# A 16384 x 2048 by 2048 x 2048 product on one Trainium2 core: the head joins the table of places, SBUF is divided by hand, chained products run by column halves

## The chip, the core and the metric

The kernel runs on one core of a Trainium2 chip. The core has five engines that run their own instruction streams: TensorE (PE, with its weight loads shown as PEld), VectorE (DVE), ScalarE (ACT), GpSimd (POOL) and SyncE (SP), which here issues nearly all DMAs. The metric is the device time of one execution in microseconds; lower is better.

## The reference

```python
def reference(x, w):          # x: 8 x 2048 x 2048, w: 2048 x 2048, float32
    cs = np.cumsum(x, axis=1)
    diff = cs - np.concatenate([np.zeros(...), cs[:, :-1, :]], axis=1)
    return np.matmul(diff, w).astype(np.float32)
```

The difference of a running sum is x again, so what is computed is x times w, with x as 16384 rows of 2048.

## The kernel before

The rows of x are 128 tiles of 128 rows. The work has a head, 31 groups of four tiles, and an end.

**The head** (lines 197 to 473) multiplies the first four tiles (PLAIN = 4) in bfloat16, directly, while w arrives. w comes in 32 slices of 128 x 1024 float32 (512 KB): `w.0.k` is the first column half of rows 128k and on, `w.1.k` the second. The four tiles of x come in 16 blocks of 256 KB, quarter q of the columns for tile r. Each quarter is cast to bfloat16 (`cast_x`, DVE), turned by 16 transposes on PE (`turn_x`) and copied to `xP` (`turned`). Each slice of w is cast into a ring of seven buffers (`taken`, ACT), and DVE takes its largest absolute value (1.21 us each). A product is one 128x128 by 128x512 matmul. The first half of w has 112 of them (7 for each k), the second 128, and `left_over` 16: one bank's worth of the result is left to the end of the head, since there are only eight banks in PSUM and the transposes need one. Ahead of all this, 7 dummy products (WARM) run on zeros. The results go from PSUM to buffers of the pool `o` (`plain_out`) and out by DMA: seven of the first half on GpSimd's queue behind the maximum over all partitions (L296), the others on SP.

When the whole of w is there, its maximum gives a scale, `uinv` (L381), and w is rewritten in place as float16 blocks: B11, B12, B21 (`block`, L392), later B22, and the differences T1 = B12 - B11, T2 = B22 - T1, T3 = B22 - B12, T4 = B21 - T2. They are operands of Winograd's form of the 2 x 2 block product, which has seven products instead of eight.

**A group** handles tiles g, g+1, g+2, g+3. Each tile is loaded in two halves (`load`, 512 KB each), weighed (`weigh`, ACT, for its scale; `mean` and `scale` on DVE, `unit` on POOL), narrowed to float16 (`narrow`, ACT) and turned by two DMA transposes (`turn`). DVE makes the sums S1 to S4. Group 0 (`group_plain`) and group 1 are special; groups 2 to 30 are alike and have 204 products each: 64 in chained products (`S2g T2`, `S2h T2`, `S3g T3`, `S3h T3`, each of 16 products that add to a pair of banks, X or Y) and five second-level products P1 to P5 of seven `slot`s (`P1.0` to `P1.6`, four products each; class `Quarters`). Within such a P, ACT copies a bank after slot 0 (`first`), slot 2 (`out2`) and slot 4 (`out4`), and DVE adds it to another (`middle`, `last`). Some right operands of the second level (Q1, Q3, Q4) pass through a buffer `flow`, filled by DVE or by DMA from a copy in DRAM. Results leave PSUM by `keep` (ACT) and `add` (DVE), and then by `put` (DMA, 512 KB).

**What sets the order.** Operations of the groups are not issued at once: `record` files each under its period (group) and a label, and `emit(places)` sorts all by `period * PERIOD + place` and then issues them. `after` ties every instruction of PE, DVE, ACT, SP and POOL to the one issued before it on the same engine, so each engine runs them in the order of the table, and waits for operands where they are late. The label's number is the role: `put2.1` is half 1 of tile g+2, `load7.1` half 1 of the next group's fourth tile, `put-1.0` the half that the group before left. The table has four columns: groups 0, 1, 2, and one for all others. The head is not in it: its instructions are issued as the code calls them, with an `emit()` between.

Memory is taken from pools: `ring`, `o` and `first` for the head, closed at its end, then `C`, `inner`, `flow` and `chain` over the same memory. An operation that first writes a new pool's buffer waits for what used those bytes in the old one.

Of the kernel before, what the change touches and what calls it, by code (L numbers as in the profile page):

```python
# [10 lines left out]
def kernel(  # L11
# [29 lines left out]
    WARM = 7  # L41
# [3 lines left out]
    PERIOD = 833  # L45
# [16 lines left out]
    uw = const.tile([P, 1], f32, name="uw")  # L62
    uinv = const.tile([P, 1], f32, name="uinv")

    waste = const.tile([P, NH], mybir.dt.uint8, name="waste")
    F = const.tile([P, 4, NH], f32, name="F")
# [3 lines left out]
    sums_at, means_at, scales_at, units_at = (  # L70
        [const.tile([P, n], f32, name=f"{name}{i}") for i in range(count)]
        for name, n, count in (("m", 2, 4), ("m1_", 1, 2), ("s", 1, 8), ("u", 1, 8))
    )
# [5 lines left out]
    def bank(i):  # L79
        return banks[i]  # L80
# [3 lines left out]
    def after(engine, ask):  # L84
        if engine in last:
            with tc.issue_after(last[engine].ins):
                said = ask()
        else:
            said = ask()
        last[engine] = said[-1] if isinstance(said, tuple) else said  # L90
        return said

# [104 lines left out]
    with tc.tile_pool(name="ring", bufs=7) as ring, tc.tile_pool(  # L197
        name="o", bufs=7
    ) as opool, tc.tile_pool(name="first", bufs=1) as first:
        xP = first.tile([P, PLAIN, KO, P], bf16, name="xP")  # L200
        eye = first.tile([P, P], bf16, name="eye")
        wmax = first.tile([P, 2 * KO], f32, name="wmax")
        wred = first.tile([P, 1], f32, name="wred")
        zeros = xP[:, 0, :KQ, :].rearrange("p k m -> p (k m)")


        def resting(k, a):
            return whole[k][:, a, 1, :]


        number = [resting(i, 1)[:, :P] for i in range(3)]
        nc.vector.memset(zeros, 0.0)
        nc.vector.memset(number[0], 1.0)
        nc.vector.tensor_tensor_scan(
            number[1], number[0], number[0], 0.0, MUL, ADD
        )
        nc.vector.transpose(number[2], number[1])
        for i in range(0, P, 32):
            own = ds(i, 32)
            nc.vector.tensor_scalar(  # L220
                eye[own, :],
                number[1][own, :],
                number[2][own, i : i + 1],
                None,
                mybir.AluOpType.is_equal,
            )

        def load_x(q, rows=range(PLAIN)):
            for r in rows:
                nc.sync.dma_start(  # L230
                    resting(KH - 1 - q, r // 2)[:, ds(r % 2 * NB, NB)],
                    x2[ds(r * P, P), ds(q * KQ * P, KQ * P)],
                )

        def cast_x(q, pairs=range(2)):
            xb = resting(q, 0).bitcast(bf16).rearrange("p (a c) -> p a c", a=2)
            for a in pairs:
                after(
                    "dve",
                    lambda: nc.vector.tensor_copy(xb[:, a], resting(KH - 1 - q, a)),  # L240
                )
            return xb


        def turn_x(xb, a, i):
            v = bank(i).bitcast(bf16)
            for k in range(2 * KQ):
                at = ds(k * P, P)
                after("pe", lambda: nc.tensor.transpose(v[:, at], xb[:, a, at], eye))
            return v  # L250

        def turned(q, a, v, engine):
            to = xP[:, ds(2 * a, 2), ds(q * KQ, KQ), :].rearrange("p r k m -> p r (k m)")
            v = v.rearrange("p (r c) -> p r c", r=2)
            if engine == "act":
                after("act", lambda: nc.scalar.copy(to, v))
            else:
                after("dve", lambda: nc.vector.tensor_copy(to, v))

        wb = {}  # L260

        def fetch(h, ko):
            wt = whole[ko % KH][:, ko // KH, h, :]
            nc.sync.dma_start(wt, w[ds(ko * P, P), ds(h * NH, NH)])

        def taken(h, ko):
            wt = whole[ko % KH][:, ko // KH, h, :]
            i = h * KO + ko
            b = wb[h, ko] = ring.tile([P, NH], bf16, name="wb")
            after("act", lambda: nc.scalar.copy(b, wt))  # L270
            after(
                "dve",
                lambda: nc.vector.tensor_reduce(
                    wmax[:, i : i + 1], wt, AX.X, MAX, apply_absolute_value=True
                ),
            )


        def here(h, r):
            return range(1 if h == 0 and r == PLAIN - 1 else 2)  # L280

        def plain(h, r, ko):
            for n in here(h, r):
                after(
                    "pe",
                    lambda: nc.tensor.matmul(  # L286
                        ps[r][n],
                        xP[:, r, ko, :],
                        wb[h, ko][:, ds(n * NB, NB)],
                        start=(ko == 0),  # L290
                        stop=(ko == KO - 1),
                    ),
                )

        def put(c, rows, columns, queue=nc.gpsimd):
            return queue.dma_start(out2[rows, columns], c)  # L296

        def plain_out(h, r):
            for n in here(h, r):
                if h == 0 or r > 0:  # L300
                    c = opool.tile([P, NB], f32, name="o")
                else:
                    c = ring.tile([P, NH], bf16, name="wb").bitcast(f32)
                after("act", lambda: nc.scalar.copy(c, ps[r][n]))  # L304
                done.append((c, ds(r * P, P), ds(h * NH + n * NB, NB)))


        for i in range(WARM):
            after(
                "pe",  # L310
                lambda: nc.tensor.matmul(
                    bank(0), zeros[:, :P], zeros, start=True, stop=True
                ),
            )
        AHEAD = 3
        done = []
        ps = [[bank(2 * r + n) for n in here(0, r)] for r in range(PLAIN)]


        loads = {2: 1, 5: 2, 9: 3}  # L320
        turns = {2: (1, 0), 3: (1, 1), 5: (2, 0), 6: (2, 1), 9: (3, 0), 10: (3, 1)}
        for ko in range(KO):
            if ko in loads:
                load_x(loads[ko])
            if ko < 2:
                load_x(0, range(2 * ko, 2 * ko + 2))
            fetch(0, ko)
        for ko in range(KO - KQ):
            if ko == 0:
                for a in range(2):  # L330
                    xb = cast_x(0, [a])
                    turned(0, a, turn_x(xb, a, 6 + a), "dve")
                    if a == 0:
                        taken(0, ko)
                    for r in (2 * a, 2 * a + 1):
                        plain(0, r, ko)
                continue
            if ko in turns:
                q, a = turns[ko]
                if a == 0:  # L340
                    xb = cast_x(q)
                v = turn_x(xb, a, 7)
                taken(0, ko)
                turned(q, a, v, "act")
            else:
                taken(0, ko)
            for r in range(PLAIN):
                plain(0, r, ko)
        for ko in range(KO - KQ, KO):
            taken(0, ko)  # L350
        for ko in range(AHEAD):
            fetch(1, ko)
        for ko in range(AHEAD):
            taken(1, ko)
        for r in range(PLAIN):
            for ko in range(KO - KQ, KO):
                plain(0, r, ko)
            plain_out(0, r)
        ps = [[bank(2 * r + n) for n in here(1, r)] for r in range(PLAIN)]
        for ko in range(KO - KQ):  # L360
            if ko >= AHEAD:
                fetch(1, ko)
                taken(1, ko)
            for r in range(PLAIN):
                plain(1, r, ko)
        for ko in range(KO - KQ, KO):
            fetch(1, ko)
        for ko in range(KO - KQ, KO):
            taken(1, ko)


        for t in (PLAIN, PLAIN + 2):
            load(t, 0)
            load(t, 1)
        emit()
        after("dve", lambda: nc.vector.tensor_reduce(wred, wmax, AX.X, MAX))
        whole_max = nc.gpsimd.partition_all_reduce(uw, wred, P, bass_isa.ReduceOp.max)
        after(
# [962 lines left out]
```

## Time and profile before

| | |
|---|---|
| median of three runs | 1460.88 us (1459.04 to 1462.82) |
| the profiled execution | 1460.01 us, span 1458.2 us |
| HBM read, written | 196.61 MB, 135.79 MB |
| DMA, busy share over the span, mean rate | 0.93 for the main queue, 273 GB/s |

A span runs from the first to the last instruction. Of each engine the profile has the busy time and, for each instruction, what released it. DMA rows show their issue on SP's queue (`SPq`); the landing is a separate time. In the table by stage, the first column is the stretch in us from the span's start.

### The profile page before, as it was taken

How to read it: one execution, taken by the hardware profiler on the slowest of the kernel's cores; microseconds unless marked ns; L12 is line 12 of the kernel's file. 1: busy time of each engine (PE TensorE's matmuls, PEld its weight loads, DVE VectorE, ACT ScalarE, POOL GpSimd, SP SyncE). 2: the span in 40 equal slices, each digit the busy share in tenths (PEclk: the TensorE clock that was granted, in tenths of full speed). 3: DMA queues.
4: the chain of work that ended last, by engine and by line, in shares of the span. 5: the costliest groups of instructions: out<-in, count | busy, mean ns of one | idle time of the engine just before them, and what ended most of it. 6: DMA issues, size and time to landing. Idle time of an engine off the chain costs nothing.

```text
span 1458.2 us, 20418 instructions
## 1 busy us (share of the span) xinstructions
PE 1440.1 (99%) x6677; PEld 652.3 (45%) x6683; DVE 1260.6 (86%) x2292; ACT 1142.9 (78%) x1742; POOL 42.8 (3%) x136
## 2 busy tenths in 40 slices
PE   8999999999999999999999999999999999999997
PEld 3444444444444444444444444444444444444443
DVE  7898988888888888888888888888888988888886
ACT  5887778887888877888878788878788878888863
POOL 0100000000000000000000000000000000000000
PEclk9999999999999999999999999999999999999999
DMA  9989999899999999999999999999999999999983
GB/s 360 367 221 264 278 271 258 281 307 250 276 273 261 281 302 261 271 270 267 286 288 267 265 275 268 296 280 265 263 276 269 306 263 277 257 269 279 313 230 125
DMA packets 355387, 398.79 MB, mean 273 GB/s; under 512 B 272272, under 2 KB 272784, under 8 KB 355152
## 3 DMA queue, kind: packets, MB, share of 16 engines
q1 hardware_dynamic: 354720, 395.65, 93.4%
q0 software_dynamic: 560, 1.84, 0.3%
q8 instruction: 52, 0.85, 0.2%
q14 instruction: 55, 0.45, 0.1%
HBM read 196.61 MB, written 135.79 MB: 228 GB/s over the span
## 4 chain that ended last, share of the span: by engine, by line
PE 93%; DMA 3%; DVE 1%; ACT 1%; issue 0%; SPq 0%; DVEq 0%; POOL 0%; ACTq 0%
PE b L541 61%; PE b L522 31%; DMA W<-in_w_dram 3%; PE b L286 1%; DVE W L392 1%; DMA out_dram<-c 1%; ACT W L577 0%; DVE c L566 0%; DMA out_dram<-o 0%; ACT o L304 0%; ACT c L555 0%; DVE b L509 0%; DVE x L509 0%; ACT xP L160 0%; ACT wb L270 0%
## 5 line engine op out<-in xcount | busy, mean ns | idle before, releaser
L522 PE MATMUL b<-W,x 128*128 128x512 f16 x2176 | 524.0, 379 | 0.0
L566 DVE SCALAR_TENSOR_TENSOR c<-b,u,c 128x512 f32<-128x512 f32 x612 | 444.9, 744 | 42.1 <-PE b L541 25.6
L541 PEld LDWEIGHTS <-inner 128*128 128x128 f16 x2700 | 264.0, 98 | 318.8 <-DVE inner L509 0.4
L541 PE MATMUL b<-W,inner 128*128 128x512 f16 x1640 | 401.9, 379 | 0.0
L555 ACT ACTIVATE c<-b,u 128x512 f32<-128x512 f32 x496 | 321.5, 687 | 29.4 <-PE b L541 9.2
L522 PEld LDWEIGHTS <-x 128*128 128x128 f16 x2176 | 212.9, 98 | 257.1 <-issue 0.7
L160 ACT ACTIVATE F<-F,s 128x1024 f16<-128x1024 f32 x246 | 282.6, 1149 | 48.9 <-DVE s L149 45.9
L541 PE MATMUL b<-W,x 128*128 128x512 f16 x1180 | 293.5, 379 | 0.3 <-ACT b L558 0.3
L128 ACT ACTIVATE waste<-F 128x1024 uint8<-128x1024 f32 x246 | 260.0, 1057 | 35.3 <-DMA F<-in_x_dram 34.1
L541 PEld LDWEIGHTS <-x 128*128 128x128 f16 x1416 | 138.6, 98 | 167.5 <-issue 0.6
L558 ACT COPY chain<-b 128x512 f32<-128x512 f32 x234 | 136.6, 584 | 93.0 <-PE b L541 91.6
L541 PE MATMUL b<-flow,inner 128*128 128x512 f16 x704 | 180.7, 379 | 0.0
L509 DVE TENSOR_TENSOR b<-b,chain 128x512 f32<-128x512 f32 x234 | 162.1, 693 | 14.9 <-ACT c L555 11.2
L558 ACT COPY b<-b 128x512 f32<-128x512 f32 x147 | 83.8, 570 | 77.4 <-PE b L541 38.7
L509 DVE TENSOR_TENSOR inner<-x,x 128x1024 f16<-128x1024 f16 (+1 forms) x180 | 91.9, 511 | 27.8 <-PE b L541 26.1
L509 DVE TENSOR_TENSOR flow<-W 128x2048 f16<-128x2048 f16 x90 | 109.6, 1218 | 0.0
L509 DVE TENSOR_TENSOR x<-x,x 128x1024 f16<-128x1024 f16 x124 | 84.8, 686 | 3.1
L541 PE MATMUL b<-inner 128*128 128x512 f16 x356 | 86.5, 379 | 0.0
L150 POOL TENSOR_SCALAR u<-m,uw 128x1 f32<-128x1 f32 x124 | 37.8, 312 | 1307.2 <-DVE m L147 1299.2
L509 DVE TENSOR_TENSOR inner<-inner 128x512 f16<-128x512 f16 x116 | 49.3, 425 | 30.0 <-PE b L541 27.9
L509 DVE TENSOR_TENSOR inner<-x,inner 128x512 f16<-128x512 f16 x118 | 49.6, 421 | 16.4 <-PE b L541 13.6
L509 DVE TENSOR_TENSOR flow<-W,inner 128x2048 f16<-128x2048 f16 (+1 forms) x33 | 37.2, 1127 | 29.5 <-PE b L541 29.5
(53 smaller groups left out, 671.1 us busy)
## 6 DMA issues: line engine op xcount, KB each, us to landing
out_dram<-c SPq DMA_DIRECT2D x248, 512.0 KB, 5.4
F<-in_x_dram SPq DMA_DIRECT2D x246, 512.0 KB, 5.8
flow<-kept SPq DMA_DIRECT2D x87, 512.0 KB, 4.3
W<-in_w_dram SPq DMA_DIRECT2D x32, 512.0 KB, 9.6
W<-in_x_dram SPq DMA_DIRECT2D x16, 256.0 KB, 7.4
x<-F SPq DMA_TRANSPOSE x246, 5.2
out_dram<-o POOLq DMA_DIRECT2D x7, 256.0 KB, 3.9
out_dram<-o SPq DMA_DIRECT2D x7, 256.0 KB, 4.7
```

What stands on the lines that cost most here:

```text
L128: lambda: nc.scalar.activation(waste, data, ABS, scale=1.0 / ROW, accum_out=m),
L150: record(f"unit{role(t)}", "pool", lambda: nc.gpsimd.tensor_scalar(u, m, uw, None, MUL))
L160: lambda: nc.scalar.activation(to, data, COPY, scale=s),
L286: lambda: nc.tensor.matmul(ps[r][n], xP[:, r, ko, :], wb[h, ko][:, ds(n * NB, NB)], start=(ko == 0), stop=(ko == KO - 1),),
L392: "dve", lambda: nc.vector.tensor_scalar(dst[k], src, uinv, None, MUL)
L509: record(label, "dve", lambda: nc.vector.tensor_tensor(dst, p, q, op))
L522: said = nc.tensor.matmul(to[n], a[k], b[k][:, n, :], start=(start and k == 0), stop=(k == KH - 1), skip_group_check=True,)
L541: said = nc.tensor.matmul(to, a[k], b[k], start=(start and k == 0), stop=(k == 3), skip_group_check=True)
L555: record(label, "act", lambda: nc.scalar.activation(c, p, COPY, scale=u))
L558: record(label, "act", lambda: nc.scalar.copy(to, p))
L566: label, "dve", lambda: nc.vector.scalar_tensor_tensor(c, p, u, c, MUL, ADD)
```

## The change

Eight things change.

1. The head is recorded too: its transposes, products, casts, loads and puts get labels (`first x.q.r`, `w.h.k`, `cast x.q.a`, `turn x.q.a`, `cast w.h.k`, `max w.h.k`, `plain.h.r.k`, `out.h.r.n`, `left over.i`, `B11.k`, ...) in period 0 and places in the table.
2. The pools in SBUF go. One tile `arena` of 46 KB per partition is divided by hand; scales and maxima share the tile `tiny`, and the unit matrix lies in `waste`.
3. WARM is 19 in place of 7.
4. A chained product was issued in four pieces of two k with both column halves; it is now issued in four pieces of four k with one column half n.
5. The last group's and the end's orders are their own: the table now is a dictionary with columns for 0, 1, 2, 29, 30 and 31, and one for all others.
6. Puts of the last group go out in halves of 256 KB.
7. All puts of the head are on SP's queue; none is on GpSimd's.
8. The load of tile 5 (`load1`) is two DMAs in place of one.

All orders in the table are new. The core of the diff:

```diff
-    WARM = 7
+    WARM = 19
-    PERIOD = 833
+    PERIOD = 1589
...
+    arena = const.tile([P, 46 * 256], f32, name="arena")
...
+    ring = [area(2 * i, 2, bf16) for i in range(7)]
+    results = [area(14 + 2 * i, 2, f32) for i in range(8)]
+    xP = area(30, 16, bf16).rearrange("p (r k m) -> p r k m", r=PLAIN, k=KO)
+    free = [area(4 * i, 4, f32).rearrange("p (n c) -> p n c", n=2) for i in (0, 1, 2, 4)]
+    S1_at = area(12, 4, f16).rearrange("p (i n c) -> p i n c", i=2, n=2)
+    rooms_at = area(20, 4, f16).rearrange("p (j c) -> p j c", c=NB)
+    inner = area(24, 16, f16).rearrange("p (j c) -> p j c", c=NB)
+    flow = area(40, 4, f16).rearrange("p (j c) -> p j c", c=NB)
+    chain = area(44, 2, f32)
...
-            own = places[min(at, 3)]
+            own = places[at] if at in places else places[None]
...
+    def result(name, p, rows, columns, u=None):
+        c = next(results_at)
+        if u is None:
+            record(f"{name}", "act", lambda: nc.scalar.copy(c, p))
+        else:
+            record(f"{name}", "act", lambda: nc.scalar.activation(c, p, COPY, scale=u))
+        done.append(
+            (f"put {name}", lambda: nc.sync.dma_start(out2[rows, columns], c))
+        )
...
-    def matmuls(label, to, a, b, ks, start):
+    def matmuls(label, to, a, b, n, ks, start):
         def some():
             for k in ks:
-                for n in range(2):
-                    said = nc.tensor.matmul(to[n], a[k], b[k][:, n, :], ...)
+                said = nc.tensor.matmul(to[n], a[k], b[k][:, n, :], ...)
             return said
-        record(label, "pe", some)
+        record(f"{label}.{n}.{ks[0] // 4}", "pe", some)
+
+    def halves_of(label, to, a, b, start):
+        return [(label, to, a, b, n, range(4 * i, 4 * i + 4), start) for n in range(2) for i in range(2)]
...
     def put(c, t, h):
+        if t < END - 4:
...
+        else:
+            for n in range(2):
+                put_half(c[:, n, :], t, h, n)
```

From the new table, in the order that it gives to each engine (labels alone):

```
SP, start:    w.0.2, w.0.0, w.0.3, first x.0.0, first x.0.1, w.0.1, first x.1.1, first x.0.2, first x.0.3,
              first x.2.1, first x.1.2, first x.1.0, w.0.4, first x.1.3, w.0.5, w.0.7, first x.2.0, ...
SP, before:   first x.0.0, first x.0.1, w.0.0, first x.0.2, first x.0.3, w.0.1, first x.1.0 to 1.3,
              w.0.2, w.0.3, w.0.4, first x.2.0 to 2.3, w.0.5 to w.0.8, first x.3.0 to 3.3, w.0.9, ...
PE, start:    warm.0 to 18, turn x.0.0, plain.0.1.0, plain.0.1.1, plain.0.0.0, turn x.0.1, plain.0.0.1,
              plain.0.0.2, plain.0.0.3, plain.0.2.0, plain.0.3.0, turn x.1.0, plain.0.1.2, ...
PE, head end: plain.1.3.15, left over.0, left over.1, A11g B11 (16 products), left over.2, A12g B21.0.0,
              left over.3, rest of A12g B21, A11h B11 and A12h B21, S1g T1, S2g T2.0.0, S2g T2.1.0, S4g B22
DVE:          uinv, B11.4, B21.7, B21.3, mean0, scale0, B12.0, B11.0, B12.2, B21.1, B11.6, B11.2, B11.1,
              mean2, scale2, B11.3, B11.7, B11.5, B21.2, B12.6, B21.4, T1.2, B21.6, B21.0, B12.3, B21.5,
              B12.1, mean1, scale1, T1.0, T1.6, T1.1, B12.5, B12.4, B12.7, C11g+V.1, T2[:4].1, T1.7,
              C11g+V.0, B22.7, T1.5, mean3, scale3, S1g, T1.3, T1.4, ...
PE, groups 3 to 28 (common column):
              P1.0, P2.0, P1.1, P1.2, P2.1, P2.2, P1.3, P2.3, P2.4, P1.4, P2.5, P1.5, P1.6, P5.0, P2.6, ...
              P5.6, P3.1, S2h T2.1.0, S2h T2.0.1, P3.2, P3.3, S2h T2.1.1, P3.4, P3.5, P4.0, P3.6, ...
ACT, there:   ... narrow6.1, keep C22h.1, keep C12h.1, P3.out2, ...
ACT, before:  ... narrow6.1, P3.out2, keep C22h.1, keep C12h.1, ...
DVE, there:   ... C22h+Y.0, in1.Q1, mean7, P2.s1, P2.s2, scale7, C22h+Y.1, (next) C21h+P4.h.0, P4.last, ...
DVE, before:  ... P2.s1, C21g+P4.g.1, C22h+Y.0, (next) C21h+P4.h.0, P2.s2, mean7, scale7, P4.last, C22h+Y.1
SP, there:    ... put2.1, load7.1, load8.0, turn5.1, turn5.0, put1.0, put1.1, ...
PE, end:      ... S3h T3.1.0, S3h T3.1.1, P4.4, P4.3, P4.5, P4.6
DVE, end:     ... C22h+Y.1, P4.last, C21g+P4.g.0, C21g+P4.g.1, C21h+P4.h.1, C21h+P4.h.0
SP, end:      ... put1.0.0, put1.0.1, put-1.0.1, put-1.0.0
```

More of the change, by code (lines that the diff above doesn't have):

```diff
@@ L195, in emit, with resting, eye_rows @@
         ops.clear()
[L197 to L220, printed above, removed]
+    def resting(k, a):
+        return whole[k][:, a, 1, :]
+    zeros = xP[:, 0, :KQ, :].rearrange("p k m -> p (k m)")
+    number = [resting(i, 1)[:, :P] for i in range(3)]
+    def eye_rows(i):
+        own = ds(i, 32)
+        record(
+            "eye",
+            "dve",
+            lambda: nc.vector.tensor_scalar(
                 eye[own, :],
@@ L295, in put @@
[L295 to L305, printed above, removed]
@@ new lines, with rest, fetch, taken @@
+    wb = {}
+    rings = iter(ring * 6)
+    def rest(h, ko):
+        return whole[ko % KH][:, ko // KH, h, :]
+    def fetch(h, ko):
+        to = rest(h, ko)
+        record(
+            f"w.{h}.{ko}", "sp", lambda: nc.sync.dma_start(to, w[ds(ko * P, P), ds(h * NH, NH)])
+        )
+    def taken(h, ko):
+        src, most = rest(h, ko), wmax[:, ds(h * KO + ko, 1)]
+        to = wb[h, ko] = next(rings)
+        record(f"cast w.{h}.{ko}", "act", lambda: nc.scalar.copy(to, src))
+        record(
+            f"max w.{h}.{ko}",
+            "dve",
+            lambda: nc.vector.tensor_reduce(most, src, AX.X, MAX, apply_absolute_value=True),
+        )
@@ new lines, in put_done, with warm @@
+    def put_done():
+        for name, ask in done:
+            record(name, "sp", ask)
+        done.clear()
+    def warm(i):
+        record(
+            f"warm.{i}",
+            "pe",
+            lambda: nc.tensor.matmul(banks[0], zeros[:, :P], zeros, start=True, stop=True),
+        )
+    for i in range(WARM):
+        warm(i)
+    AHEAD = 3
+    done = []
+    ps = [[banks[2 * r + n] for n in here(0, r)] for r in range(PLAIN)]
+    loads = {2: 1, 5: 2, 9: 3}
+    turns = {2: (1, 0), 3: (1, 1), 5: (2, 0), 6: (2, 1), 9: (3, 0), 10: (3, 1)}
@@ L446 @@
-        narrow(PLAIN + 2)
-        emit()
-        turn(PLAIN + 2)
-        emit()
-        finish_row(2)
-        for k in range(4, KH):
-            block(B21, 1, 0, k, "dve")
-        finish_row(3)
-        for k in range(KH):
-            block(B12, 0, 1, k, "dve")
-        left_over(bank(2))
-        for c, rows, columns in done:
-            after("sp", lambda: put(c, rows, columns, nc.sync))
-        weigh(PLAIN + 1)
-        emit()
-        scale_of(PLAIN + 1)
-        emit()
-        narrow(PLAIN + 1)
@@ L464 @@
-        emit()
-        turn(PLAIN + 1)
-        emit()
-        load(PLAIN + 3, 0)
-        emit()
-        load(PLAIN + 3, 1)
-        emit()
-        for k in range(KH):
-            after("dve", lambda: nc.vector.tensor_tensor(T1[k], B12[k], B11[k], SUB))
+                    )
+                return said
+            record(f"left over.{i}", "pe", some)
+        result("out", p, ds((PLAIN - 1) * P, P), ds(NB, NB), uw)
+    for k in range(4):
+        block("B11", B11, 0, 0, k, "dve")
+    weigh(PLAIN)
@@ new lines, with load_5 @@
+    scale_of(PLAIN)
+    for k in range(4, KH):
+        block("B11", B11, 0, 0, k, "dve")
+    narrow(PLAIN)
+    turn(PLAIN)
+    finish_row(0)
+    for k in range(4):
+        block("B21", B21, 1, 0, k, "dve")
+    weigh(PLAIN + 2)
+    scale_of(PLAIN + 2)
+    finish_row(1)
+    x5 = area(30, 8, f32)
+    where[PLAIN + 1] = [x5[:, :NH], x5[:, NH:]]
+    for i in range(2):
+        def load_5(i=i):
+            return nc.sync.dma_start(
+                x5[:, ds(i * NH, NH)], x2[ds((PLAIN + 1) * P, P), ds(i * NH, NH)]
+            )
+        record(f"load1.{i}", "sp", load_5)
@@ new lines, with difference @@
+    put_done()
+    narrow(PLAIN + 2)
+    turn(PLAIN + 2)
+    finish_row(2)
+    for k in range(4, KH):
+        block("B21", B21, 1, 0, k, "dve")
+    finish_row(3)
+    for k in range(KH):
+        block("B12", B12, 0, 1, k, "dve")
+    left_over(banks[2])
+    put_done()
+    weigh(PLAIN + 1)
+    scale_of(PLAIN + 1)
+    narrow(PLAIN + 1)
+    turn(PLAIN + 1)
+    load(PLAIN + 3, 0)
+    load(PLAIN + 3, 1)
+    def difference(k):
+        record(f"T1.{k}", "dve", lambda: nc.vector.tensor_tensor(T1[k], B12[k], B11[k], SUB))
@@ L476 @@
+    for k in range(KH):
+        difference(k)
     class Part:
@@ L896, in group @@
             )
-            for i in range(4)
+            for one in halves_of(name, to, a, b, False)
         ]
```

396 lines of the change are left out of this document (173 added, 223 removed), and 513 rows, old and new, of the table places.

## The prediction

> **What bounds it now.** I read the busy shares first, then a table of the busy time by stage, then TensorE's timeline, the waits of the head, and the last microseconds.
>
> ```profile
> span 1458.2 us, 20418 instructions
> PE 1440.1 (99%) x6677; PEld 652.3 (45%) x6683; DVE 1260.6 (86%) x2292; ACT 1142.9 (78%) x1742; POOL 42.8 (3%) x136
> ...
> 6.50:38.60 32.10, 27.97 (x151) 13.63 (x155) 25.16 (x26) 21.63 (x23) 0.00 (x0) 1.00 1.03 402
> 38.60:75.60 37.00, 36.44 (x163) 16.24 (x166) 31.67 (x40) 30.82 (x41) 5.90 (x10) 1.00 0.94 341
> ...
> 160.00:1425.00 1265.00, 1265.00 (x5862) 573.34 (x5861) 1100.89 (x2023) 1012.10 (x1564) 31.60 (x115) 1.00 0.96 274
> ```
>
> The columns of a stage are its length, then busy time (count) of PE, PEld, DVE, ACT, POOL, then clock, DMA share, GB/s. From 160 to 1425 us TensorE never pauses: 1265.00 of 1265.00, one product per 0.2159 us (1265/5862 is 0.2158). An order of the other engines can gain nothing there; it can only lose. By the loops, group 0 has 224 products, group 1 has 216 and 29 groups have 204, 6356 in all.
>
> ```profile
> 1.18 3.17 PE L311 MATMUL b<-xP 128*128 128x512 bf16 x7 [1.18 <-DVE xP L212]
> 11.89 4.17 PE L286 MATMUL b<-wb,xP 128*128 128x512 bf16 x10 [0.79 <-DVE xP L258]
> 38.62 33.50 PE L286 MATMUL b<-wb,xP 128*128 128x512 bf16 x147 [0.35 <-ACT wb L270]
> 91.77 3.61 PE L522 MATMUL b<-W,inner 128*128 128x512 f16 x16 [2.03 <-ACT W L577]
> ```
>
> Up to 38.6 us TensorE follows the arriving data. From 38.62 it is dense until 75.62, where group 0 starts. It pauses once more, 2.03 us ahead of `S1g T1`, at 91.77. Behind that, 6356 - 64 products of 0.2159 are 1358.4 us, which ends at 1450.2; the trace ends its last product at 1449.44 + 1.03 = 1450.47. So three places can pay: the time before 91.77, some 0.3 us behind it, and the 7.8 us after the last product.
>
> ```profile
> POOL u L150 <- issue: 7.9, 1, 7.9
> DVE m L147 <- POOL u L150: 3.1, 1, 3.1
> ...
> 82.91 3.15 DMA out_dram<-o
> 86.06 0.03 ACTq L555
> ...
> 88.59 3.12 ACT W L577 x3
> 91.71 0.06 issue
> ```
>
> The 2.03 us have a history. VectorE stood 3.1 us at 72.3 for `unit0`, which on GpSimd was queued behind the puts of the first rows. The first `keep C11g` then waited for a put out of the pool whose memory it takes over (82.91 to 86.06), and B22, T2 and S1g came late.
>
> **The head, step by step.** Landings first. The trace gives, in queue order, `w.0.0` at 1.05 MB and 7.28 us, `w.0.2` at 3.67 MB and 13.75, `w.0.5` at 6.29 MB and 21.22, `w.0.9` at 9.44 MB and 29.58:
>
> ```profile
> 7.28 1.04 ACT L270 CAST wb<-W 128x1024 bf16<-128x1024 f32 x1 [5.28 <-DMA W<-in_w_dram]
> 13.75 1.04 ACT L270 CAST wb<-W 128x1024 bf16<-128x1024 f32 x1 [2.90 <-DMA W<-in_w_dram]
> 21.22 1.04 ACT L270 CAST wb<-W 128x1024 bf16<-128x1024 f32 x1 [0.77 <-DMA W<-in_w_dram]
> 29.58 1.04 ACT L270 CAST wb<-W 128x1024 bf16<-128x1024 f32 x1 [2.06 <-DMA W<-in_w_dram]
> ```
>
> I put the new queue on this curve (0.40 MB/us past its end). Three slices of w now go ahead of x, so the second block of x is at 2.10 MB and 9.8 us instead of 5.8: the first transposes start at 10.5 (cast 0.69) and not 6.5. In exchange each quarter of x finds its w there: x quarter 1 complete at 17.5, quarter 2 at 24.7, quarter 3 at 31, `w.0.15` (12.58 MB) at 37.4. Taking the new TensorE order piece by piece (cast of w 1.05, `turned` 1.0 on ScalarE or 0.69 on VectorE, eight transposes 0.61), I get pauses of 2.3 us between 10.5 and 18.8 and none later, and 42.7 us as the time when all 112 products of the first half and 4 of the second are through: 116 x 0.2159 = 25.0, plus 64 transposes 4.9, plus 2.3, is 32.2 from 10.5. There remain 124 + 16 (`left over`), 30.2 us, and some 0.5 us while ScalarE drains the first banks: 73.4. `left over` is now mixed with group 0's first 64 products (13.8 us), so `S1g T1` can start at **87.2**.
>
> Can VectorE follow? It gets `uinv` at 60.1 as before, since the same 20.97 MB come first. In the new order, up to the last operand of that product, stand 24 blocks of B11, B21, B12 at 0.68 (5.42/8), one of B22 0.7, eight differences at 0.61, two adds 1.4, four means with scales 1.6, S1g 0.7, and 0.5 of waiting for `weigh0`: 26.0, so 86.1. It is ready 1.1 us before TensorE. The hole of 3.1 us is gone because the puts leave GpSimd for SP, and `keep C11g` lies on two places of the ring, out of which nothing is put. The head gains 91.77 - 87.2 = **4.6 us**. Bounds: TensorE dense from 10.5 gives 6.9; if x, coming 4 us later, costs all that the order regains, and only the stall goes, 2.0; if VectorE is late too, -1.
>
> What I cost at nothing: twelve more dummy products (0.45 each by the 3.17 us of seven, 5.4 us) lie before 10.5, when TensorE would wait for x; without that cover they cost 5.4. Column halves keep 16 products and 16 weight loads for each chained product. `load1` in two parts, and puts of 15 results on SP, are 16 more issues of 0.33 there, 5.3 us over the head, while VectorE and TensorE go on; uncovered, the first group's turns come that much later. With wmax, means and eye in shared tiles, only overlapping columns should wait.
>
> [...] Products took 0.42 us each at 11.89 (4.17 us for ten) and 0.216 later. [...]
>
> **Steady state.** I followed one period of the new order with these durations (group start 0, TensorE dense). The nearest calls: `P3.out2` now stands behind two keeps on ScalarE, ends at 28.1, and `P3.4` needs it at 28.5; `P2.first` ends at 3.1 for `P2.2` at 4.3; `P5.first` at 15.6 for 16.4. All in time, so 0, and 0.2 gained of the 0.3.
>
> **The end.**
>
> ```profile
> 1442.83 11.15 SPq L584 DMA_DIRECT2D out_dram<-c  x5
> ...
> 1449.64 2.07 DVE L566 SCALAR_TENSOR_TENSOR c<-b,u,c 128x512 f32<-128x512 f32 x3 [2.85 <-PE b L541]
> 1451.63 0.69 DVE L509 TENSOR_TENSOR b<-b,chain 128x512 f32<-128x512 f32 x1
> 1452.22 1.40 DVE L566 SCALAR_TENSOR_TENSOR c<-b,u,c 128x512 f32<-128x512 f32 x2
> ...
> DMA to landing us min/median/max: 2.6/3.3/5.8
> ```
>
> Five adds and a `last` run after the last product, until 1453.6; the put of 512 KB lands at 1458.2. In the new order `P4.last` and two adds come before: behind the product that precedes the last stand three adds, 0.70 apart, ending 1.65 us after the last product; then a put of 256 KB, 0.1 and 3.3 (the median of the end's puts): 5.05 instead of 7.77, **2.7 us** gained; 3.4 and 0.5 if landing takes 2.6 or 5.5.
>
> **Sum.** 1458.2 - 4.6 - 0.2 - 2.7 = 1450.7 of span. The profiled execution took 1460.0 with its 1458.2, 1.8 more: 1452.5. It lies 0.9 below the median of the three runs: **1453.4 us**. Its own range, from the bounds of head and end: 1450 to 1458.
>
> **Rivals.** (1) The head returns only the stall or less: x later eats what the denser middle gains. For it: the first useful product comes 4 us later. Against it: products ready per MB. With 0 to 2 from the head, 1456 to 1458. Chance 0.17. (2) TensorE dense from the first transposes: 6.9 + 0.3 + 3.0 gives 1450.7; 0.10. (3) The clock halves again between the dummies and the first x, and products run at 0.42 until 16 us: nine products and sixteen transposes in that stretch, 2.8 us, so 1456.2. The dummies would end between 7 and 10.7, a gap of at most 3.5; 0.05. [...] (4) Slower: `mean7` now stands on VectorE ahead of `P2.s1`, `P2.s2`, `C22h+Y.1` and `C21h+P4.h.0`; before it stood behind all but the third. It waits for `weigh7.1`, hence for `load7.1`. Issued at 36 in the period, that lands at 41.6 by the median 5.6, in time; at the longest landing of loads in the steady state, 8.5, `P2.first` ends at 4.85 and `P2.2` wants 4.3: 0.55 us. From 7.9 us of landing on it decides; in all 26 periods of the common table it is 14.3 us, 1467.7. For it: DMA is busy 0.96 of the time. Against: the median. 0.13, of which 0.02 for a milder form of 0.3 us each (1461). (5) The regions of the one stretch of SBUF are kept apart less finely than the tiles, so the head waits as before and only the end gains: 1458.1; 0.02.
>
> **How the numbers follow.** My forecast has 0.53, (1) to (5) the rest. Repeated runs spread by 3.8 us, so about 0.3% (4.4 us, below 1456.5) is what can be told from no change. Faster: 0.51 of the forecast, 0.05 of (1), 0.10 of (2) and 0.03 of (3), 0.69. Slower: 0.11 of (4). No change: the remaining 0.20. The range 1448.5 to 1461 leaves out the 0.11 above and some 0.05 below.
>
> **What would show it.** `S1g T1` near 87 and no idle time of TensorE ahead of it; no wait of DVE for POOL of 3 us; products at 0.216 us before 16 us; the stage from 160 to 1400 still at 100%; the end 5 us behind the last product. A share below 99.9% in the steady stage, with waits on the `first` or `out2` copies, would make the prediction wrong.

## The result, and the profile after

The changed kernel takes 1468.55 us (median, 1467.62 to 1470.78) against 1462.15 (1459.04 to 1463.43) of the kernel before on the same chip: ratio 1.0049, interval 1.0036 to 1.0062. It is slower by 0.5%, where 1453.4 was forecast. The profiled execution took 1470.8 us with a span of 1469.0. That is the slowest of its six, and the profile of the kernel before lies 2.1 us below that kernel's median: the two spans differ by 10.8 us, the medians by 6.4. What is read from their traces below is of these two executions.

Head and end came as forecast. TensorE's timeline of the changed kernel (start, length, engine and line, operation, and in brackets the idle time ahead and what ended it):

```profile
2.13 7.12 PE L338 MATMUL b<-arena 128*128 128x512 bf16 x19 [2.13 <-DVE arena L229]
11.20 0.93 PE L260 MATMUL b<-waste,W 128*128 128x128 bf16 x8 [1.95 <-DVE W L251]
12.91 2.74 PE L302 MATMUL b<-arena 128*128 128x512 bf16 x6 [0.79 <-DVE arena L270]
...
33.72 36.85 PE L302 MATMUL b<-arena 128*128 128x512 bf16 x170
...
87.68 3.62 PE L529 MATMUL b<-W,arena 128*128 128x512 f16 x16
...
1462.89 1.03 PE L551 MATMUL b<-W,x 128*128 128x512 f16 x4
```

`S1g T1` (the row at 87.68) starts 4.1 us earlier than before, with no idle time ahead, and the last product ends at 1463.92, 5.05 us before the span does. So some 7 us were won outside the steady state and 18 us lost inside it, which gives the 10.8 us between the spans. The table by stage has the loss (columns as in the prediction: length, then busy time and count of PE, PEld, DVE, ACT, POOL, then clock, DMA share, GB/s):

```profile
6.50:38.60 32.10, 29.37 (x167) 14.73 (x166) 25.25 (x28) 20.57 (x22) 0.00 (x0) 0.89 1.02 389
38.60:75.60 37.00, 37.00 (x174) 16.72 (x172) 34.82 (x45) 33.00 (x44) 2.05 (x3) 1.00 0.96 353
160.00:1425.00 1265.00, 1250.93 (x5779) 565.06 (x5778) 1080.93 (x1995) 989.30 (x1552) 46.87 (x113) 1.00 0.97 270
```

From 160 to 1425 us TensorE is busy 1250.93 of 1265.00 and issues 5779 products instead of 5862. The 83 missing products, at 0.2159, are 17.9 us. DMA is busy 0.97 instead of 0.96 of the time, and moves 270 GB/s instead of 274. To place the idle time I matched the records of each engine with the table's order, and summed what lies between the starts of two products beyond 0.2159 us: 18.1 us behind 88 us, of which 12.9 ahead of `P5.3` (17 groups, at most 1.36) and 4.1 ahead of `P5.2` (4 groups). The waits of TensorE and ScalarE, summed over the span (total us, times, longest), name the same two, in the second and third row:

```profile
ACT arena L565 <- DMA out_dram<-arena: 85.0, 60, 3.4
...
PE b L551 <- DMA arena<-kept: 10.1, 13, 1.2
PE b L551 <- ACT b L568: 3.4, 3, 1.5
```

`arena<-kept` is here nearly all `in5.t21`, the block that is brought back from DRAM into `flow` for `P5.3`. L568 is the copy `P5.first`. The first row is new in size: ScalarE stands 85.0 us at `keep`s (L565) whose buffer is still being put to DRAM, where the kernel before shows 2.3 us in 5 waits.

One group shows both (engine rows of a timeline; SPq is SP's DMA queue; the rows left out are other engines' work):

```profile
798.00 5.75 SPq L187 DMA_TRANSPOSE x<-F  x2
...
803.80 0.57 SPq L584 DMA_DIRECT2D out_dram<-arena  x1
...
804.20 1.03 PE L551 MATMUL b<-arena,x 128*128 128x512 f16 x4
804.42 0.42 SPq L130 DMA_DIRECT2D F<-in_x_dram  x1
...
805.25 0.61 SPq L639 DMA_DIRECT2D arena<-kept  x1
...
807.89 0.69 ACT L565 ACTIVATE arena<-b,tiny 128x512 f32<-128x512 f32 x1 [0.99 <-DMA out_dram<-arena]
...
812.36 1.02 PE L551 MATMUL b<-arena 128*128 128x512 f16 x4 [1.10 <-DMA arena<-kept]
```

In order: `turn7.0` and `turn7.1`; `put3.1`; `P1.6`, the last reader of `flow`; `load10.0`; `in5.t21`, issued as soon as `P1.6` is through; `keep C11h.0`, which waits until `put3.1` has landed; `P5.3`, which waits 1.10 us for `in5.t21`. Around this place the two orders are

```
SP, before: put3.1, load8.1, turn7.0, turn7.1, (next) in5.t21, load10.0, put-1.0, load6.1
SP, after:  load8.1, turn7.0, turn7.1, put3.1, load10.0, (next) in5.t21, load6.1, put-1.0
PE, before: P1.6, P2.5, P2.6, S2g T2 (2 pieces), P5.0, S2g T2 (2), P5.2, P5.1, P5.3
PE, after:  P1.6, P5.0, P2.6, S2g T2 (3 pieces), P5.1, P5.2, P5.3, S2g T2 (1)
```

Two things changed here. The new order has seven pieces between `P1.6` and `P5.3` instead of nine, so `P5.3` is due (what the pieces between take without a pause) 5.88 us after `P1.6` ends instead of 7.61. And `in5.t21` has a load and a put just ahead of it: it lands 6.24 us after `P1.6` ends (median of groups 6 to 26, 4.82 to 7.20; 4.64 in the kernel before). `put3.1` is issued 5.27 us after its data are there (median), because SP issues `turn7.0` and `turn7.1` first. What takes the time is not their wait for `narrow7` but the issue itself: SP is at the two transposes for 5.75 us in the row at 798.00, and in the mean of groups 6 to 26 they take 1.45 and 3.30 of the 5.23 us, with 0.36 us in which SP issues nothing. A plain DMA takes SP 0.3 to 0.6 us there, for the most part.

### The profile page after: what moved, and what is told of

The parts are those of the page before. It is cut to its first block, busy times and chain, and to the rows that moved or that the text cites. A ratio compares the mean times of both kernels' runs of the same rounds, so it can differ in the third digit from the quotient of the medians.

```text
span 1469.0 us, 20458 instructions
## 1 busy us (share of the span) xinstructions
PE 1445.0 (98%) x6695; PEld 653.9 (45%) x6695; DVE 1254.9 (85%) x2292; ACT 1129.0 (77%) x1742; POOL 55.1 (4%) x129
## 4 chain that ended last, share of the span: by engine, by line
PE 88%; DMA 9%; DVE 1%; ACT 1%; issue 0%; SPq 0%; DVEq 0%; ACTq 0%
PE b L551 54%; PE b L529 29%; DMA arena<-kept 6%; PE b L302 4%; DMA out_dram<-arena 2%; DMA W<-in_x_dram 1%; DVE arena L576 0%; DMA F<-in_x_dram 0%; DVE b L517 0%; PE b L260 0%; DVE arena L517 0%; PE b L430 0%; SPq L187 0%; ACT F L170 0%; ACT arena L565 0%
## 5 line engine op out<-in xcount | busy, mean ns | idle before, releaser
L576 DVE SCALAR_TENSOR_TENSOR arena<-b,tiny,arena 128x512 f32<-128x512 f32 x612 | 447.7, 745 | 71.3 <-PE b L551 41.3
L551 PEld LDWEIGHTS <-arena 128*128 128x128 f16 x2700 | 263.9, 98 | 336.5 <-issue 20.5
L565 ACT ACTIVATE arena<-b,tiny 128x512 f32<-128x512 f32 x496 | 324.7, 687 | 109.3 <-DMA out_dram<-arena 85.0
L551 PE MATMUL b<-W,arena 128*128 128x512 f16 x1640 | 398.5, 379 | 3.5 <-ACT b L568 3.4
L170 ACT ACTIVATE F<-F,tiny 128x1024 f16<-128x1024 f32 x246 | 282.8, 1150 | 11.1 <-DVE tiny L159 7.6
L138 ACT ACTIVATE waste<-F 128x1024 uint8<-128x1024 f32 x246 | 260.5, 1059 | 29.0 <-DMA F<-in_x_dram 27.0
L551 PE MATMUL b<-arena 128*128 128x512 f16 x1060 | 258.4, 379 | 10.4 <-DMA arena<-kept 10.1
L568 ACT COPY arena<-b 128x512 f32<-128x512 f32 x294 | 168.7, 585 | 88.5 <-PE b L551 85.5
L517 DVE TENSOR_TENSOR b<-b,arena 128x512 f32<-128x512 f32 x294 | 201.4, 693 | 39.4 <-ACT arena L568 36.7
L568 ACT COPY b<-b 128x512 f32<-128x512 f32 x147 | 84.3, 574 | 75.4 <-PE b L551 37.4
L517 DVE TENSOR_TENSOR arena<-W 128x2048 f16<-128x2048 f16 (+1 forms) x98 | 112.9, 1154 | 20.1 <-PE b L551 19.6
L517 DVE TENSOR_TENSOR arena<-x,x 128x1024 f16<-128x1024 f16 (+1 forms) x180 | 91.8, 511 | 25.4 <-PE b L551 18.2
L517 DVE TENSOR_TENSOR x<-x,x 128x1024 f16<-128x1024 f16 x124 | 82.7, 685 | 1.1
L517 DVE TENSOR_TENSOR arena<-x,arena 128x512 f16<-128x512 f16 x118 | 47.6, 421 | 19.0 <-PE b L551 18.0
L517 DVE TENSOR_TENSOR arena<-arena 128x512 f16<-128x512 f16 x116 | 48.7, 420 | 6.0 <-PE b L551 0.5
```

The source lines that it names most:

```text
L138: lambda: nc.scalar.activation(waste, data, ABS, scale=1.0 / ROW, accum_out=m),
L170: lambda: nc.scalar.activation(to, data, COPY, scale=s),
L517: record(label, "dve", lambda: nc.vector.tensor_tensor(dst, p, q, op))
L551: said = nc.tensor.matmul(to, a[k], b[k], start=(start and k == 0), stop=(k == 3), skip_group_check=True)
L565: record(label, "act", lambda: nc.scalar.activation(c, p, COPY, scale=u))
L568: record(label, "act", lambda: nc.scalar.copy(to, p))
```

## The experiments

e1 to e8 are the changed kernel with places of its table overwritten, e10 to e12 are e9 with one or two more. "Idle" is TensorE's, summed as above; it includes what products at half clock take beyond 0.2159 us, some 8 us in e7, 6 in e12, 3 in e1, e3 and e6, 2 in e2, and nothing in the others. Times are medians; the kernel before took 1461.4 beside e1 to e4, 1460.9 beside e5 to e8, and 1462.0 beside e9 to e12.

**e1: load10.0 behind in5.t21.**

```diff
+    places[None]['load10.0'] = places[2]['load10.0'] = 2030
+    places[1]['load10.0'] = 1872
```

> The changed kernel with one DMA moved: load10.0 is issued right behind in5.t21 and no longer right ahead of it. In the changed kernel in5.t21 lands 6.3 us after its issue (median, up to 7.2; before 4.3), P5.3 can stand 5.84, and TensorE lost 12.9 us ahead of P5.3 in 17 groups and 4.1 us ahead of P5.2 in 4. Theory Q (what is in flight ahead of in5.t21 sets its landing): 512 KB fewer ahead, at 0.40 MB/us 1.3 us sooner, 5.0 us; P5.3's stall falls below 1.5, P5.2's stays: 1456 to 1458 us. Rival A (the 16 DMA engines are simply full, 0.97 of the time, in any order): the landing stays above 6 and the time within 2 us of 1468.5.

1499.76 us, ratio to before 1.0264 (1.0248 to 1.0279). `in5.t21` now lands 4.01 us after `P1.6`, and no idle time is left at `P5.3`. But the idle time is 49.3 us, 30.3 of it at `P5.4`. In group 2 `weigh6.0` stands ahead of its load here and in e3, so one row tile is scaled by other rows' mean. The waits of e1:

```profile
ACT waste L138 <- DMA F<-in_x_dram: 80.1, 55, 6.0
...
PE b L551 <- ACT arena L568: 31.2, 27, 5.2
```

ScalarE now stands at `weigh6.0` (L138) for `load10.0`, and `P5.out2` (L568), which `P5.4` needs, is queued behind it. So the landing follows what is ahead in the queue, and by more than the 1.3 us expected; the time does not, since the DMA that gave way was itself just in time.

**e2: put3.1 ahead of load8.1. e3: e1 and e2 together.**

```diff
+    places[None]['put3.1'] = 1757
+    places[2]['put3.1'] = 1621
+    places[1]['put3.1'] = 1404
```

> The changed kernel with one put moved: put3.1 is issued ahead of load8.1 and the two turns of tile 7, as in the kernel before, instead of behind them. C11h takes the buffer that put3.1 empties, so keep C11h.0 waits for that put, and narrow4.1, P5.first and P5.2 behind it. Theory Q: in5.t21 has 512 KB fewer ahead, lands after some 5.0 us, P5.3's 12.9 us nearly go; and the chain from put3.1 to P5.2 goes too, 4.1 us: 1451 to 1454 us. If only the buffer matters and not the queue: 1464. Rival A: 1466 to 1469, with P5.2's stall the only gain.

> Both moves. Theory Q: no stall of TensorE in groups 2 to 30, 18.1 us less than the changed kernel's 1468.5: 1450 to 1453 us, which is 0.6 to 0.8% below the kernel before. Rival A: no better than 1464.

e2: 1479.61 us, 1.0120 (1.0092 to 1.0149), idle 29.0, now at `P5.2` (8.6), `P5.1` (7.7) and `S2g T2.1.0` (7.1). e3: 1495.76 us, 1.0236 (1.0221 to 1.0251), idle 43.4. In e2 SP stands at `put3.1` for `C22h+Y.1`, and `load8.1` and the turns behind it come later for `weigh4.1`, `mean4` and the sums: `load8.1` lands 0.21 us before `P1.6` ends instead of 2.09 (medians), and `weigh4.1` waits 1.5 us for it. The wait that e2 was aimed at is gone: `keep C11h.0` finds its buffer free 4.2 us before it starts. But `in5.t21` lands only 0.43 us sooner than in the changed kernel, after 5.81 us; e3, with `load10.0` behind as well, has 3.79. Both missed what was expected of the time.

**e4: one more piece ahead of P5.3.**

```diff
+    places[None]['P5.3'] = 460
```

> The changed kernel with one piece of TensorE's order exchanged in groups 3 to 28: S2g T2.1.1 ahead of P5.3 instead of behind it; no DMA moves. Theory W (between P1.6, which frees the buffer flow, and P5.3 only seven pieces are left, where there were nine): the landing that P5.3 can stand rises by one piece, 0.86 us, to 6.70; by the landings of the changed kernel 2.9 us of its 12.9 stay: 1458 to 1460 us, with in5.t21 landing at 6.3 as now. If the landing stretches with the room that it gets (rival A): above 1464.

1472.14 us, 1.0067 (1.0046 to 1.0088): not faster, where 1458 to 1460 was expected. The idle time at `P5.3` fell from 12.9 to 2.3 us, as the run of pieces says (due 6.74 us after `P1.6`, landed after 6.49). But 6.1 us appeared at `P3.0`, and the sum is 20.2. In the changed kernel `P3.0` starts 0.69 us (at the least 0.08) after `keep C12g.0` has freed its bank. That points at the idle time at `P5.3` as what had let ScalarE catch up; it was not tested by itself.

**e5 to e7: whose order is at fault.** In the column for groups 3 to 28 the sequence of an engine is replaced by that of the kernel before: in e5 of all five engines, in e6 of SP alone, in e7 of all but SP. Group 28 keeps the new column (in e5 and e7 with `P1.first` a little later).

```diff
+    places[28] = dict(places[None])
+    places[None] = {
...
+    }
```

> The changed kernel with its own head, its own SBUF layout, its own halves and its own end, but in groups 3 to 27 all five engines follow the order of the kernel before (each chained product's four pieces stand where its four pieces stood). Theory O (the loss is the new order of the steady groups): the 18.1 us of TensorE idle go and nothing comes for them, 1468.5 - 18.1 = 1450.4, and some 1 to 2 us for the groups at the ends that keep their order: 1449 to 1454. Rival H (the loss is in the layout or the halves: other buffers or coarser waits make the DMAs land later whatever the order): at least half of the idle stays, 1460 or more.

> The changed kernel; in groups 3 to 27 only SP's DMAs follow the order of the kernel before, TensorE, VectorE, ScalarE and GpSimd keep the new order. Theory S (SP's order alone makes the loss): in5.t21 lands in about 4.1 us, no idle ahead of P5.3, 1450 to 1456. Theory O in its stricter form (the five orders fit only together; a DMA moved for one reader is late for another): idle at P5.4 to P5.6 or P5.2 as in the two runs that moved one DMA, 1475 or more.

> The counterpart: in groups 3 to 27 the four engines follow the order of the kernel before, SP keeps the new one. in5.t21 again has four DMAs just ahead of it and lands in about 6.3 us; nine pieces of 0.86 us (7.8 us) stand between P1.6 and P5.3 in this order, so theory W (the shorter run of pieces between P1.6 and P5.3 is what makes the late landing cost time) says no idle ahead of P5.3 and 1450 to 1456. Theory S says the loss stays, about 1468. Theory O in its stricter form says idle elsewhere, 1475 or more.

e5: 1458.38 us, 0.9984 (0.9975 to 0.9993); idle 5.6 us, all of it in groups 3, 28 and 29, where two orders meet, and none in groups 4 to 27. That is the changed kernel's layout, halves, head and end, so these cost nothing in the steady state, and rival H falls. The time is 4 us above the range given, because the seams cost more than the 1 to 2 us allowed. e6: 1537.13 us, 1.0521 (1.0504 to 1.0539), idle 85.7, of which 37.4 at `P1.6`, 16.6 at `P5.4` and 15.5 at `P3.0`; `in5.t21` lands early there, 3.69 us after `P1.6`, and `P5.3` waits 0.6 us in all. e7: 1527.59 us, 1.0442 (1.0415 to 1.0469), idle 75.7. SP's old order with the others' new one, or the reverse, is far worse than either whole order: in this split the orders fit only together, as the stricter theory O said. The waits of e7:

```profile
ACT arena L565 <- DMA out_dram<-arena: 86.7, 30, 4.6
...
PE b L551 <- DVE arena L517: 40.5, 25, 2.8
...
PE b L551 <- DMA arena<-kept: 13.8, 17, 2.2
```

The loss sits at `P5.2` (46.4 us), behind the `keep` that waits for `put3.1`, and at `P4.4` (19.9 us), which in most groups waits for `in4.Q3`, another block out of DRAM (the third row). `P5.3` has 1.8 us, but e7 does not test theory W: `in5.t21` lands 7.56 us after `P1.6` (median), in 11 of 26 groups later than the 7.61 that nine pieces cover, and it is the wait at `P5.2`, ahead of `P5.3`, that hides it.

**e8: e1, and weigh6.0 behind P5.out2.**

```diff
+    places[None]['weigh6.0'] = 476
+    places[2]['weigh6.0'] = 284
```

> e1 (load10.0 behind in5.t21) and weigh6.0 moved on ScalarE from ahead of P5.out2 to behind it. If the reading of e1 is right (its 49 us of idle came because the load, 4 us later, held weigh6.0, and weigh6.0 held P5.out2 and P5.out4 behind it in ScalarE's order), P5.4 to P5.6 no longer wait, P5.3 does not wait either, and what is left is P5.2's 4 us and little more: 1452 to 1458. The rival (DMA has no slack in any order): idle of 15 us or more at other pieces, 1465 or more.

1479.24 us, 1.0120 (1.0105 to 1.0135). The reading of e1 holds: the idle time at `P5.4` to `P5.6` is gone but for 0.6 us (49.3 to 27.3 us in all). But 13.7 us are now at `P3.0` and 3.3 at `P5.2`. The rival's number was right: in the new order another wait stands close behind each one that is taken away.

**e9: the old order up to the seams.** Groups 28 and 29 too follow the order of before, as do the first pieces of group 30, and two DMAs of group 2 are moved:

```diff
+    places[2].update(
+                'put3.1': 1621, 'load10.0': 2029.01,
...
+    places[30].update(
+                'P1.0': -353, 'P1.1': -157, 'P2.0': -156.99, 'C21h+P4.h.0': -135.97,
...
+    places[None] = {
...
+    places[29] = {k: places[None][k] for k in places[29]}
```

> e5 carried on to the seams: group 28, group 29 and the first pieces of group 30 also follow the order of the kernel before, and put3.1 and load10.0 of group 2 stand as there; head, layout, halves and end are the changed kernel's. In e5 the seams held 5.6 us of idle TensorE (2.6 at P5.2, 1.6 at P1.2, the rest 0.5 and less) and groups 4 to 27 none. Theory O: the seams' idle goes too, 1458.4 - 5.6 = 1452.8, within 1451 to 1455: about 8 us under the kernel before, the gain of head (4.1) and end (2.7) at last. Rival: another seam moves the idle on to groups 29 and 30, 1456 to 1459.

1453.74 us, 0.9944 (0.9932 to 0.9957) of the kernel before: faster than both. The steady state is whole again:

```profile
160.00:1425.00 1265.00, 1264.84 (x5859) 572.95 (x5858) 1101.14 (x2022) 1010.43 (x1567) 34.64 (x113) 1.00 0.96 273
```

And the same place of its timeline, with `P1.6`, `in5.t21`, `load10.0` and `P5.3`:

```profile
794.97 1.03 PE L551 MATMUL b<-arena,x 128*128 128x512 f16 x4
...
796.91 0.53 SPq L639 DMA_DIRECT2D arena<-kept  x1
797.49 0.42 SPq L130 DMA_DIRECT2D F<-in_x_dram  x1
...
803.60 1.03 PE L551 MATMUL b<-arena 128*128 128x512 f16 x4
```

**e10, e11: one and two DMAs ahead of in5.t21, on e9.** e9 has no idle time, so here one cause can be added by itself. In the table, `load10.0` goes to 2028.99, for e11 with `put-1.0` at 439.99 behind it (`in5.t21` is at 440).

```diff
-            'turn7.1': 1794.03, 'load10.0': 2029.01,
+            'turn7.1': 1794.03, 'load10.0': 2028.99,
```

> e9 and load10.0 put ahead of in5.t21 in every group, as the new order has it. in5.t21 stood 2.90 us (at the least 2.35) before P5.3 needed it in e5, with a landing of 4.28; a 512 KB transfer ahead of it should add what it takes at 274 GB/s, 1.9 us, so 6.2. Theory Q with its threshold (the wait appears only where landing exceeds the run of pieces between P1.6 and P5.3; 7.2 us here): no idle at P5.3, time within 1.5 us of e9. Rival (any DMA moved ahead costs, because the queue has no slack): idle of 10 us or more, e9 + 10.

> e9 and two transfers, load10.0 and put-1.0, ahead of in5.t21. Landing 4.28 + 2 x 1.9 = 8.1, over the 7.2 us that the pieces cover by 0.9: theory Q says that P5.3 now waits some 0.5 to 0.9 us in most of the 27 groups, 12 to 25 us of idle there, and the time is e9 + 12 to + 25. Rival (landing does not follow what is in flight ahead): P5.3 still does not wait, e9 + less than 3.

e10: 1455.81 us, 0.9958 (0.9945 to 0.9972), idle 2.5. e11: 1481.87 us, 1.0132 (1.0113 to 1.0151), idle 23.6, of which 21.6 at `P5.3` in 22 groups. The wait of TensorE for the block, first in e10, then in e11:

```profile
PE b L551 <- DMA arena<-kept: 0.9, 2, 0.6
```

```profile
PE b L551 <- DMA arena<-kept: 17.9, 20, 1.9
```

From the end of `P1.6` to the landing it takes 4.68 us in e9, 6.80 in e10 and 8.63 in e11 (medians), about 2 us for each of the two DMAs, and `P5.3` is due after 7.61. Part of the second step is SP's own time: from its issue to its landing `in5.t21` takes 4.32, 6.18 and 7.02 us, and SP issues it 0.36, 0.56 and 1.28 us after `P1.6` ends. One transfer ahead costs 1.6 us at `P5.3`, two cost 21.6: a threshold, as theory Q has it. e10 is 2.1 us over e9, somewhat more than the 1.5 given; e11 is 28.1 over it in the medians, where up to 25 was given, and 22.7 in the profiled executions.

**e12: put3.1 behind the turns, on e9.**

```diff
-            'put3.1': 1794, 'load8.1': 1794.01, 'turn7.0': 1794.02, 'turn7.1': 1794.03,
+            'load8.1': 1794.01, 'turn7.0': 1794.02, 'turn7.1': 1794.03, 'put3.1': 1794.035,
```

> e9 and put3.1 behind load8.1, turn7.0 and turn7.1, as the new order has it, still ahead of in5.t21. In e5 put3.1 landed 1.18 us (at the least 0.40) before keep C11h.0 wanted its buffer, and in the changed kernel ScalarE stood there 1.1 us in each group. Theory B (ScalarE's wait at keep C11h.0 makes P5.first and so P5.2 late): put3.1 goes out some 2 us later, ScalarE waits at keep C11h.0 in every group, P5.first loses its 0.96 us of margin, and P5.2 waits: idle of 5 to 25 us at P5.2, e9 + 5 to + 25. Rival (ScalarE makes it up before P5.first, or SP gets rid of the put no later): e9 + less than 3.

1509.96 us, 1.0322 (1.0278 to 1.0366), idle 57.6, of which 50.7 at `P5.2`. The direction is theory B's, the size more than twice what it gave. Its waits:

```profile
ACT arena L565 <- DMA out_dram<-arena: 96.8, 36, 4.2
...
PE b L551 <- DVE arena L517: 46.0, 28, 2.8
```

`put3.1` goes out 5.69 us after its data are there instead of at once, ScalarE stands 3.4 us at `keep C11h.0` in each group, VectorE stands behind it at `C11h+P2.h.0` 2.4 us, and `P5.s1` and `P5.s2` (L517) are queued behind that add. So the wait reaches `P5.2` by VectorE, not by `P5.first` as expected. e12 also shows a put alone ahead of `in5.t21`: `put3.1` is issued 1.03 us before it, and it lands 4.93 us after `P1.6`, 0.25 later than in e9, where `load10.0` in e10 made it 2.1 later.

## Why the prediction was wrong, step by step

**The head** was right: 4.1 us gained for 4.6, with the first transposes at 11.20 for 10.5 and `S1g T1` at 87.68 for 87.2. The 3.1 us wait of VectorE for GpSimd is gone; the longest is now 0.6. **The end** was right: 5.05 us behind the last product. e9, which has this head and this end and an undisturbed steady state, takes 1453.74 us, the forecast of 1453.4 within its spread.

**The steady state** was the wrong step: "All in time, so 0". It is 18.1 us. I had followed the copies and sums of one period, but not the DMAs that the new order moves past each other. Of the three calls listed, `P3.out2` came as reckoned (0.37 us ahead of `P3.4`, median, for 0.4) and `P2.first` earlier (1.82 us ahead for 1.2); `P5.first` did not: 0.38 us ahead of `P5.2` in place of 0.8, and 0.05 where `P5.2` waits for it. Three things of that step failed.

(1) `in5.t21` was not among the calls. A cost of nothing takes it to land as before, 4.64 us after `P1.6`, though the new order puts `put3.1` and `load10.0` right ahead of it and takes two pieces (1.7 us) out of its cover. Landing after 6.24 us against 5.88 due is the 12.9 us at `P5.3`. Either change alone fits: e10 has a late landing (6.80) under nine pieces and 1.6 us at `P5.3`; e1 has seven pieces and the early landing (4.01), and next to nothing there; e11 shows the threshold. Of the two DMAs it is the load that counts: without `load10.0` ahead (e1) the landing falls by 2.23 us, without `put3.1` (e2) by 0.43. Why a load ahead delays it more than a put is not shown.

(2) `put3.1` behind the turns was costed at nothing. Its delay goes on through `keep C11h.0`, and e12 shows by itself that it makes `P5.2` late, 50.7 us in the order of before. In the new order it gives the 4.1 us at `P5.2`, by the trace: in the four groups `keep C11h.0` waits 1.2 to 3.4 us for the put, and `narrow4.1` and `P5.first` follow it without a pause. e2 could not confirm this by the time: `P5.first` comes late there for another reason, the wait of `weigh4.1` for `load8.1` (8.6 us at `P5.2`). `put2.1` is late in the same way: ScalarE waits for it at `keep C21h.0` for 2.0 us in each group of the changed kernel, and not in e9, where the buffer is free 0.67 us before it is wanted. Part of the delay of `put3.1` is SP's wait for the operand of a turn ahead of it: in e12 SP issues nothing for 1.66 us (mean of groups 6 to 26) until `narrow7.0` has ended, with the data of `put3.1` ready. In the changed kernel that part is 0.36 us, and the issue of the two transposes is 4.75.

(3) I took the margins to be separate. They are not: e1, e2, e4 and e8 each took away most of the wait they were aimed at, and 18 to 49 us of idle time stood elsewhere. With DMA busy 0.97 of the time, and SP, ScalarE and VectorE each taking their work in order, a place that was given up in these four was another operand's margin.

**The rivals.** (4) had the sign and not the mechanism: `P2.2` has 1.35 us and more of margin to its operands in groups 6 to 26. That its 1467.7 lies close to the measured 1468.55 is luck. The order of VectorE there was also misread, in the list ahead of the prediction too: places below zero belong to the group ahead, so that `mean7` is followed by the next group's `C21h+P4.h.0`, and then by `P2.s1`, `P2.s2`, `scale7` and `P4.last`. (1), (2) and (5) did not come: head and end returned their share, and the regions of the one stretch held nothing up. (3) came in the profiled execution, with half the clock up to 18.2 us, but `S1g T1` was late by 0.5 us at the most, not by the 2.8 of its price (1456.2 less 1453.4). What makes the clock fall there no run shows; it fell in nine of the thirteen profiles with this head. Of the signs to look for, the last one did its work: a steady share of 98.9% instead of 100%, with waits on a `first` copy and on a DMA.

What stays open: which of the places that ScalarE and VectorE have in the new order take the margin at `P3.0` and the sums was not separated, no run shows why the issue of a transpose takes SP 1.2 to 3.9 us, and no small edit of the new order was found that removes its idle time; only the exchange of the whole order did.

## What to carry to other kernels

Where a table moves work, list for each DMA the instruction that waits for it and the pieces between issue and need, and count what stands ahead of it in the queue; here a load of 512 KB ahead was about 2 us and a put 0.25 (e12) to 1.8 (e11), nearly free up to the cover (1.6 us at `P5.3` in e10) and paid in most groups beyond it (21.6 us in 22 groups of e11). Count also, for a transfer whose data are ready, what the issuing engine still does for those ahead: here `put3.1` went out 5.27 us after its data were there (median), with 4.75 us for the issue of two transposes ahead and 0.36 without an issue (means), and in e12 5.69 us after, with 1.66 of waiting for `narrow7.0`; for the buffer that it frees ScalarE stood 3.4 us in each group of e12. When an order that is already dense is exchanged for a new one, compare whole orders, and try the old order under the new layout first: SP's order of one with the engines' order of the other was 4 to 5% slower than either.

## What the runs showed that was not expected

The clock after the dummies. All thirteen profiles of kernels with the changed head run the same 19 dummies from 2.13 us on, in 5.80 to 7.12 us, and start the first transposes at 11.1 to 12.1, after an idle time of 1.95 to 3.74 us. The granted clock (third number from the end) from 12.9 to 15.5 us was, in the changed kernel and in e9:

```profile
12.90:15.50 2.60, 2.58 (x7) 0.94 (x8) 1.23 (x2) 0.00 (x0) 0.00 (x0) 0.50 1.05 389
```

```profile
12.90:15.50 2.60, 2.03 (x15) 1.06 (x16) 1.50 (x3) 0.32 (x1) 0.00 (x0) 1.00 1.08 366
```

In e6, e8, e9 and e10 it stayed at 1.00, after idle times of 2.15 to 2.71 us. In the other nine it fell to half for 3.4 or 6.8 us, over by 16.0 to 18.9 us, even after the shortest, 1.95 in the changed kernel; so the length of the idle time alone did not decide. (The column counts a time without a record as 1.00: in the kernel before the record begins at 15.6 us, 3.7 us into the row at 11.89, and products took 0.42 us until then.) It cost little that can be seen: `S1g T1` started at 86.7 to 87.7 us in the four with the full clock and at 86.6 to 88.2 in the nine, in the mean 0.2 us later. That the arriving data set the pace there is the likely reason; it was not tested.

Between 88 us and the last product, in the fourteen profiles together, the clock fell to half 15 times, mostly for 3.4 us, and each time behind a wait of TensorE of 2.19 us or more. Two of the 17 waits of that length were not followed by it (2.21 us in e7, 2.51 in e12), and none of the 102 waits between 1.0 and 2.04 us was.
